# The attention scores' second pass on half the array's rows, both components at once, with the order of four engines written out

## The chip, the cores and the metric

The kernel runs on one core of one Trainium2 chip. The metric is the time of one execution in microseconds on the device; the median of the runs counts. TensorE (PE) multiplies matrices into PSUM, VectorE (DVE) and ScalarE (ACT) read PSUM, GpSimd (POOL) works on SBUF alone, and SyncE (SP) issues most transfers. Each engine has its own queue and takes its instructions in order; semaphores tie the queues together.

## What is computed

The reference is one encoder layer. The change touches its differential attention: four heads, each with two components c of 64 query and key features, 2048 tokens, values of 128 features.

```python
def block(args):
    q_blk, start = args
    ...
    bias = -slopes[:, None, None] * dist
    s = jnp.einsum('bhcqd,bhckd->bhcqk', q_blk, k).astype(jnp.float32) * scale
    p = jax.nn.softmax(s + bias[None, :, None], axis=-1)
    a = p[:, :, 0] - lam[None, :, None, None] * p[:, :, 1]
    return jnp.einsum('bhqk,bhkd->bhqd', a.astype(v.dtype), v)
```

Around it stand the input projection, a retention branch, the output projection with a residual and a two-layer MLP; none of these is edited.

## The kernel before, in words

Numbers are carried as a high and a low part, both of the type fp32r. A product of two such numbers is made of the high-high, high-low and low-high terms.

The attention stage handles 64 tiles i of 128 queries, 16 to a head; two tiles make a group g of 256 queries. Each tile goes through a pipeline of functions that is called slot by slot, four slots to a tile, in the loop at the end of `encoder`:

- `load_keys` (L971) brings a head's keys into `ka`, for each component the 64 rows of the high part in partitions 0 to 63 and those of the low part in 64 to 127. `load_group` (L993) brings the queries: `qa` holds the high part in both halves of the partitions, `qb` the low part in both halves.
- `scores` (L1023) makes, in each of a tile's four slots, the scores of one component c against 1024 keys: two matmuls on `qa` (L1042), which give high-high and high-low in one pass over 128 rows, and two on `qb` (L1043), low-high and low-low. DVE then adds the distance bias and takes the running minimum of a row (L1047; the queries are negated, so that the minimum belongs to the largest score), and after a component's second half ACT takes the exponential with its sum (L1059).
- `combine` (L1062) makes the ratio of the two sums times lambda on DVE (L1068 to L1070), and has POOL scale the second component (L1074) and add it to the first (L1075), 1024 keys at a time.
- `turn` (L1228) transposes the combined weights of tile i-2, a quarter per slot: four PE transposes into a PSUM tile `pa` (L1236), then `split_psum`: ACT writes the high part (L55), DVE the low part (L56).
- `weigh` (L1241) multiplies values and transposed weights for a group, two key tiles per slot, three matmuls each (L36 to L38 in `mm3`), into the PSUM tile `po`; after a group's eighth slot ACT copies `po` to `oT` (L1254).
- `turn_back` (L1257) transposes `oT` back into a `pa` buffer (called `pz`), scales it on ACT (L1265) and stores it.

In a slot the loop (L1272) calls `scores` for tile i, `turn` for tile i-2, `weigh` for the group of tiles i-4 and its neighbour, in even tiles' slot 1 `turn_back`, and in slot 3 `combine`. PE's order is the order of these calls (`manual_schedule` with PE alone); DVE, ACT and POOL are ordered by the planner. Of the eight PSUM banks the scores have two tiles of two banks, `po` two tiles and `pa` two.

The first two tiles (LEAD) are scored inside the retention stage before (`lead_scores`, L1080), on one-bank tiles between the retention's own matmuls: some of these use 64 rows of the array (`ret.scores`, L532, shown as 64*128), some 64 columns (`ret.within` L548, `ret.across` L560, shown as 128*64). There PE, DVE and ACT follow the order of the calls.

Of the kernel before, what the change touches and what calls it, by code (L numbers as in the profile page):

```python
# [8 lines left out]
F32 = mybir.dt.float32  # L9
# [8 lines left out]
P = 128  # L18
# [567 lines left out]
def encoder(ctx: ExitStack, tc: tile.TileContext, a: dict, out: bass.AP, dbg=None):  # L586
# [406 lines left out]
    def load_group(g):  # L993
        h, qs = g // (S // QG), g % (S // QG) * QG
        qa = kp_.tile([P, 2, QG], F32R, tag="qa", name="qa")
        qb = kp_.tile([P, 2, QG], F32R, tag="qb", name="qb")
        for t, s in ((qa, qh_d), (qb, ql_d)):
            for half in range(2):
                d = nc.sync.dma_start(
                    t[half * 64 : half * 64 + 64].bitcast(F32),  # L1000
                    s[h][:, qs : qs + QG].rearrange("(c d) q -> d c q", d=64).bitcast(F32),
                )
# [20 lines left out]
    def scores(i, slot, banks):  # L1023

        c, hf = divmod(slot, 2)
# [4 lines left out]
        if slot == 0:  # L1030
            tiles[i] = dict(p=[], l=[])
        if hf == 0:
            tiles[i]["p"].append(hp.next([P, S], F32, "p"))
            tiles[i]["nm"] = kp_.tile([P, 4], F32, tag="nm", name="nm", bufs=8)
        p, nm = tiles[i]["p"][c], tiles[i]["nm"]
        ql = slice(qi * P, qi * P + P)
        w = 1024 // len(banks)
        for b, sc in enumerate(banks):
            for o in range(0, w, 512):
                k0 = hf * 1024 + b * w + o  # L1040
                r = ka[:, c, k0 : k0 + 512]
                nc.tensor.matmul(sc[:, o : o + 512], qa[:, c, ql], r, start=True, stop=False)  # L1042
                nc.tensor.matmul(sc[:, o : o + 512], qb[:, c, ql], r, start=False, stop=True)  # L1043
            n = hf * len(banks) + b
            k0 = hf * 1024 + b * w
            b0 = k0 + S - P - qt * P
            nc.vector.tensor_tensor_reduce(  # L1047
                out=p[:, k0 : k0 + w],
                in0=sc[:],
                in1=bias[:, b0 : b0 + w],  # L1050
                scale=1.0,
                scalar=nm[:, n - 1 : n] if n else 3.0e38,
                op0=ALU.add,
                op1=ALU.min,
                accum_out=nm[:, n : n + 1],
            )
        if hf == 1:
            l = kp_.tile([P, 1], F32, tag="l", name="l", bufs=12)
            nc.scalar.activation(p[:], p[:], AF.Exp, bias=nm[:, n : n + 1], scale=-1.0, accum_out=l[:])  # L1059
            tiles[i]["l"].append(l)  # L1060

    def combine(i):  # L1062

        g, qi = divmod(i, 2)
        h = i // NT
        ps_, ls_ = tiles[i]["p"], tiles[i]["l"]
        ratio = kp_.tile([P, 1], F32, tag="ratio", name="ratio", bufs=6)
        nc.vector.reciprocal(ratio[:], ls_[1][:])  # L1068
        nc.vector.tensor_scalar(ratio[:], ratio[:], ls_[0][:], nlam[:, h : h + 1], op0=ALU.mult, op1=ALU.mult)  # L1069
        nc.vector.reciprocal(groups[g]["rl"][:, qi : qi + 1], ls_[0][:])  # L1070
        for k2 in range(2):
            p0, p1 = (t[:, k2 * 1024 : (k2 + 1) * 1024] for t in ps_)
            e = nc.vector if k2 == 0 and i == NI - 1 else nc.gpsimd
            e.tensor_scalar(p1, p1, ratio[:], 1.0, op0=ALU.mult, op1=ALU.mult)  # L1074
            e.tensor_tensor(out=p0, in0=p0, in1=p1, op=ALU.add)  # L1075
# [2 lines left out]
    LEAD = 2  # L1078

    def lead_scores(n):  # L1080
        i, slot = divmod(n, 4)
        scores(i, slot, [ret.bank([P, 512], "sc") for _ in range(2)])
        if slot == 3:
            combine(i)


# [134 lines left out]
    with ExitStack() as ph:  # L1221
        pools.append(ph.enter_context(pool(tc, "att_l", 2, side="right")))
        ap2 = ph.enter_context(pool(tc, "att_a", 2, side="right"))
        ps_s = ph.enter_context(pool(tc, "ps_as", 2, PSUM))
        ps_v = ph.enter_context(pool(tc, "ps_av", 2, PSUM))
        ps_t = ph.enter_context(pool(tc, "ps_at", 2, PSUM))

        def turn(i, k4):  # L1228
            g, qi = divmod(i, 2)
            p0 = tiles[i]["p"][0]  # L1230
            if qi == 0:
                groups[g]["a"][k4] = [ap2.tile([P, 4, QG], F32R, tag=n, name=n, bufs=7) for n in ("aTh", "aTl")]
            pa = ps_t.tile([P, 4, P], F32, tag="pa", name="pa")
            for j in range(4):
                kt = k4 * 4 + j
                nc.tensor.transpose(pa[:, j], p0[:, kt * P : (kt + 1) * P], ident[:])  # L1236
            qq = slice(qi * P, qi * P + P)
            th, tl = groups[g]["a"][k4]
            split_psum(nc, th[:, :, qq], tl[:, :, qq], pa[:])

        def weigh(g, slot):  # L1241

            h, qs = g // (S // QG), g % (S // QG) * QG
            vh, vl = heads[h]["v"]
            if slot == 0:
                groups[g]["po"] = ps_v.tile([P, QG], F32, tag="po", name="po")
# [5 lines left out]
            if slot == 7:  # L1252
                oT = ap2.tile([P, QG], F32, tag="oT", name="oT")
                nc.scalar.activation(oT[:], po[:], AF.Copy)  # L1254
                groups[g]["oT"] = oT

        def turn_back(g):  # L1257
            h, qs = g // (S // QG), g % (S // QG) * QG
# [8 lines left out]
            nc.scalar.dma_start(os.rearrange("(t p) d -> p t d", p=P), ot[:])  # L1267

        LT, LV = 2, 4
        ph.enter_context(tc.manual_schedule(engines={mybir.EngineType.PE}))  # L1270
        load_values(0)
        for i in range(LT, NI):  # L1272
            for slot in range(4):
                if slot == 0 and i % NT == 0 and i < NI - 4:
                    hh = (i + NT - 1) // NT
                    with tc.issue_after(groups[8 * hh - 4]["loaded"].ins):
                        load_keys(hh)
                        load_values(hh)
# [6 lines left out]
                j = i - LV  # L1285
                if 0 <= j:
# [23 lines left out]
        def ws(*slots):  # L1310
            for slot in slots:
                weigh(g - 1 + slot // 8, slot % 8)

        places = (hp.next([P, 2, DM], F32R, "wo") for _ in range(6))
        parts = [norms(tt, eg[:, 2], eg[:, 2]) for tt in (0, 4)]
        turn(NI - 2, 0)
        turn(NI - 2, 1)
        ws(0, 1)
        turn_back(g - 2)
        combine(NI - 1)  # L1320
        ws(2, 3)
        ph.enter_context(tc.manual_schedule(engines=ENGINES))
        turn(NI - 2, 2)
        next(parts[0])
        ws(4)
# [336 lines left out]
```

## Time and profile before

| | |
|---|---|
| median of 3 runs | 2817.68 us |
| lowest and highest | 2817.52 and 2819.99 us |
| profiled execution, time | 2819.93 us |
| profiled execution, span of its instructions | 2818.2 us |
| mean granted TensorE clock | 0.982 |
| attention stage, first and last score matmul in it | about 799 to 1339 us after the start |

Times inside the profile count from its first instruction. In its rows stand the engine, the line of the kernel, what is written from what, the shape (rows*columns of the array, then the moving operand) and, in groups, the busy time, the mean duration of one in ns, and the idle time before them with what ended it. Matmul durations overlap: what one costs is the distance between starts.

### The profile page before, as it was taken

To read this page: it belongs to the slowest core of one execution; us is meant where nothing else is said; L and a number is where in the kernel's file an instruction comes from. 1 tells how busy PE (TensorE), PEld (TensorE's weight loads), DVE (VectorE), ACT (ScalarE), POOL (GpSimd) and SP (SyncE) were. 2 spreads that over 40 slices of the span, in tenths; PEclk is the share of its full clock that TensorE was granted. 3 is DMA by queue.
4 is the path that set the end of the run, shared out by engine and by line. 5 is a ranking of instruction groups with operands and counts; after the bars stand their busy time and mean duration, and the time that the engine had idled before them with its cause. 6 is when DMAs were issued, how large, how long until landed. Compare 5 with 4: busy or idle time off the path is not lost.

```text
span 2818.2 us, 41052 instructions
## 1 busy us (share of the span) xinstructions
PE 2716.7 (96%) x15488; PEld 2332.3 (83%) x15488; DVE 1906.4 (68%) x2883; ACT 1298.4 (46%) x1844; POOL 1329.9 (47%) x768
## 2 busy tenths in 40 slices
PE   6998999998889999999899999999999999999999
PEld 4898989997778888888777788888888888888887
DVE  7888864787779999999888466665556435435542
ACT  5344422343467777777533245544445332222221
POOL 4235232513357777888454366765565104323320
PEclk8999999999899999999999999999999999999999
DMA  3665673259433222221378768776445848755471
GB/s 127 186 202 159 233 283 113 90 190 261 120 89 79 63 73 67 69 98 53 133 226 274 272 219 256 243 262 243 157 149 181 288 170 302 274 190 178 158 246 45
DMA packets 361030, 494.51 MB, mean 175 GB/s; under 512 B 23168, under 2 KB 257152, under 8 KB 352640
## 3 DMA queue, kind: packets, MB, share of 16 engines
q1 hardware_dynamic: 338608, 466.71, 50.5%
q10 hardware_dynamic: 21648, 20.98, 2.2%
q0 software_dynamic: 576, 4.19, 0.4%
q8 instruction: 122, 2.00, 0.3%
q14 instruction: 76, 0.62, 0.1%
HBM read 315.64 MB, written 176.16 MB: 175 GB/s over the span
## 4 chain that ended last, share of the span: by engine, by line
PE 79%; DVE 7%; DMA 2%; issue 1%; ACT 1%; POOL 1%; SPq 0%; ACTq 0%; DVEq 0%; POOLq 0%
PE ps L38 11%; PE ps L36 11%; PE ps L37 11%; PE p L38 7%; PE p L36 7%; PE p L37 7%; PE pa L1236 4%; PE sc L1042 4%; PE sc L1043 4%; PE po L36 2%; PE po L38 2%; PE po L37 2%; DVE kvs L511 1%; PE mm L38 1%; PE mm L37 1%
## 5 line engine op out<-in xcount | busy, mean ns | idle before, releaser
L37 PE MATMUL p<-wl,ah 128*128 128x512 f32 x896 | 348.5, 389 | 0.0
L36 PE MATMUL p<-wh,ah 128*128 128x512 f32 x896 | 348.4, 389 | 0.0
L293 POOL TENSOR_TENSOR s<-raw 128x1024 f32<-128x1024 f32 x58 | 147.2, 2539 | 372.1 <-DMA raw<-in_w_in 102.8
L334 DVE TENSOR_TENSOR c<-ps,c 128x512 f32<-128x512 f32 x360 | 238.4, 684 | 116.1 <-PE ps L38 112.5
L50 DVE TENSOR_TENSOR wl<-s,wh 128x1024 fp32r<-128x1024 f32 x120 | 194.8, 1625 | 172.9 <-ACT wh L44 172.8
L1075 POOL TENSOR_TENSOR p<-p 128x1024 f32<-128x1024 f32 x127 | 303.5, 2415 | 0.1
L44 ACT ACTIVATE ah<-ra 128x1024 fp32r<-128x1024 f32 x112 | 112.6, 1052 | 412.7 <-PE p L37 410.8
L1059 ACT ACTIVATE p<-p,nm 128x2048 f32<-128x2048 f32 x128 | 256.9, 2007 | 36.8 <-DVE nm L1047 35.7
L50 DVE TENSOR_TENSOR ah<-ra,ah 128x1024 fp32r<-128x1024 f32 x76 | 103.4, 1396 | 218.8 <-ACT ah L44 218.8
L1485 POOL TENSOR_TENSOR c<-c 128x512 f32<-128x512 f32 x128 | 196.5, 1560 | 111.3 <-ACT c L1488 109.5
L38 PE MATMUL p<-wh,ah 128*128 128x512 f32 x608 | 236.5, 389 | 0.0
L1546 POOL TENSOR_TENSOR t<-br 128x1024 f32<-128x1024 f32 x32 | 77.3, 2417 | 335.9 <-DMA br<-in_w_mlp 172.2
L44 ACT ACTIVATE wh<-s 128x1024 fp32r<-128x1024 f32 x120 | 126.6, 1057 | 208.3 <-PE ps L37 107.5
L1042 PE MATMUL sc<-ka,qa 128*128 128x512 f32 x512 | 207.5, 405 | 3.2 <-ACT yt L575 2.7
L1074 POOL TENSOR_SCALAR p<-p,ratio 128x1024 f32<-128x1024 f32 x127 | 141.9, 1130 | 143.3 <-DVE ratio L1069 110.5
L1043 PE MATMUL sc<-ka,qb 128*128 128x512 f32 x512 | 203.0, 397 | 0.0
L37 PEld LDWEIGHTS p<-wl,ah 128*128 128x128 f32 x896 | 168.2, 188 | 35.0
L36 PEld LDWEIGHTS p<-wh,ah 128*128 128x128 f32 x896 | 168.2, 188 | 34.9
L55 ACT ACTIVATE aTh<-pa 128x512 fp32r<-128x512 f32 x256 | 151.0, 591 | 81.8 <-PE pa L1236 80.6
L1047 DVE CUSTOM_DVE_ANT_0 p<-sc,bias,nm 128x1024 f32<-128x1024 f32 (+1 forms) x136 | 167.7, 1233 | 22.6 <-PE sc L1043 21.0
L1236 PEld LDWEIGHTS pa<-ident,p 128*128 128x128 f32 x1024 | 120.3, 141 | 64.6 <-issue 30.2
L56 DVE TENSOR_TENSOR aTl<-pa,aTh 128x512 fp32r<-128x512 f32 x256 | 170.3, 686 | 3.8 <-DMA vh<-vhd 3.0
(376 smaller groups left out, 8131.2 us busy)
## 6 DMA issues: line engine op xcount, KB each, us to landing
br<-in_w_mlp SPq DMA_DIRECT2D x88, 512.0 KB, 5.5
raw<-in_w_mlp SPq DMA_DIRECT2D x32, 1024.0 KB, 5.9
raw<-in_w_in SPq DMA_DIRECT2D x28, 1024.0 KB, 5.9
xt<-in_x SPq DMA_DIRECT2D x20, 512.0 KB, 5.8
q<-rqd SPq DMA_DIRECT2D x16, 512.0 KB, 10.1
qa<-qhd SPq DMA_DIRECT2D x64, 128.0 KB, 3.0
qb<-qld SPq DMA_DIRECT2D x64, 128.0 KB, 3.0
ua11d<-c SPq DMA_DIRECT2D x32, 256.0 KB, 3.5
```

Of the source, the lines that this page charges most:

```text
L36: nc.tensor.matmul(out, ah, bh, start=first, stop=False)
L37: nc.tensor.matmul(out, ah, bl, start=False, stop=False)
L38: nc.tensor.matmul(out, al, bh, start=False, stop=last)
L44: nc.scalar.activation(hi, src, AF.Copy)
L50: e.tensor_tensor(out=lo, in0=src, in1=hi.bitcast(F32), op=ALU.subtract)
L334: nc.vector.tensor_tensor(out=o[:], in0=x0[:], in1=x1[:], op=op)
L1042: nc.tensor.matmul(sc[:, o : o + 512], qa[:, c, ql], r, start=True, stop=False)
L1043: nc.tensor.matmul(sc[:, o : o + 512], qb[:, c, ql], r, start=False, stop=True)
L1059: nc.scalar.activation(p[:], p[:], AF.Exp, bias=nm[:, n : n + 1], scale=-1.0, accum_out=l[:])
L1075: e.tensor_tensor(out=p0, in0=p0, in1=p1, op=ALU.add)
L1236: nc.tensor.transpose(pa[:, j], p0[:, kt * P : (kt + 1) * P], ident[:])
L1485: nc.gpsimd.tensor_tensor(out=u[n][:], in0=u[x0][:], in1=u[x1][:], op=op)
```

## The change

- Keys: for component 1 the halves are exchanged, so that its high part lies in partitions 64 to 127 (and the low part in 0 to 63). Component 0 stays.
- Queries: `qb` now holds the low part once, component 0 in partitions 0 to 63 and component 1 in 64 to 127, loaded by one transfer.
- `scores` handles both components of 1024 keys at once, in slots 0 and 2 only. The first pass is as before, over 128 rows. The second pass uses 64 rows of `qb` and of `ka`, component 0 the lower and component 1 the upper ones, alternating; it makes low-high alone, and the low-low term is gone.
- The exponentials are a function of their own (`exps`): component 1 in slot 3, component 0 in slot 1 of the next tile, followed there by `combine`. The reciprocal for the ratio (`inverse`) comes in slot 0 of the next tile, the ratio's multiplication moves from DVE to POOL, and the reciprocal `rl` moves into `turn`.
- `turn` is one slot later; in slots 0 and 2 the low part on DVE is called only after the scores.
- PSUM: `pa` has three buffers; the two `po` are the halves of one tile `pos` in one bank. The copy to `oT` is a function `away`, called at the end of an odd tile's slot 3, behind that tile's `exps(i, 1)`.
- DVE, ACT and POOL also follow the order of the calls through the whole stage.

```diff
         for c in range(2):
-            rs = slice(c * 64, c * 64 + 64)
-            d = nc.sync.dma_start(ka[0:64, c].bitcast(F32), kh_d[h][rs, :].bitcast(F32))
-            nc.sync.dma_start(ka[64:128, c].bitcast(F32), kl_d[h][rs, :].bitcast(F32))
+            rs, os = slice(c * 64, c * 64 + 64), slice(64 - c * 64, 128 - c * 64)
+            nc.sync.dma_start(ka[rs, c].bitcast(F32), kh_d[h][rs, :].bitcast(F32))
+            nc.sync.dma_start(ka[os, c].bitcast(F32), kl_d[h][rs, :].bitcast(F32))
...
+        for c, sc in enumerate(banks):
             for o in range(0, w, 512):
-                k0 = hf * 1024 + b * w + o
-                r = ka[:, c, k0 : k0 + 512]
-                nc.tensor.matmul(sc[:, o : o + 512], qa[:, c, ql], r, start=True, stop=False)
-                nc.tensor.matmul(sc[:, o : o + 512], qb[:, c, ql], r, start=False, stop=True)
+                nc.tensor.matmul(sc[:, o : o + 512], qa[:, c, ql], ka[:, c, k0 + o : k0 + o + 512], start=True, stop=False)
+        for o in range(0, w, 512):
+            for c, sc in enumerate(banks):
+                rs = slice(c * 64, c * 64 + 64)
+                nc.tensor.matmul(sc[:, o : o + 512], qb[rs, 0, ql], ka[rs, c, k0 + o : k0 + o + 512], start=False, stop=True)
...
-        nc.vector.tensor_scalar(ratio[:], ratio[:], ls_[0][:], nlam[:, h : h + 1], op0=ALU.mult, op1=ALU.mult)
-        nc.vector.reciprocal(groups[g]["rl"][:, qi : qi + 1], ls_[0][:])
+        ratio = tiles[i]["r"]
+        nc.gpsimd.tensor_scalar(ratio[:], ratio[:], ls_[0][:], nlam[:, h : h + 1], op0=ALU.mult, op1=ALU.mult)
...
-        ps_v = ph.enter_context(pool(tc, "ps_av", 2, PSUM))
-        ps_t = ph.enter_context(pool(tc, "ps_at", 2, PSUM))
+        ps_v = ph.enter_context(pool(tc, "ps_av", 1, PSUM))
+        pos = ps_v.tile([P, 2, QG], F32, tag="po", name="po")
+        ps_t = ph.enter_context(pool(tc, "ps_at", 3, PSUM))
...
-        ph.enter_context(tc.manual_schedule(engines={mybir.EngineType.PE}))
+        ph.enter_context(tc.manual_schedule(engines=ENGINES | {mybir.EngineType.Pool}))
...
-                if i >= LEAD:
-                    scores(i, slot, [ps_s.tile([P, 1024], F32, tag="sc", name="sc")])
-                if 0 <= i - LT:
-                    turn(i - LT, slot)
+                low, (t, k4) = [], divmod(4 * (i - LT) + slot - 1, 4)
+                if t >= 0:
+                    turn(t, k4, low)
                 j = i - LV
+                if 0 < j and j % 2 == 0 and slot == 1:
+                    turn_back(j // 2 - 1)
+                if slot % 2 == 0:
+                    scores(i, slot // 2, [ps_s.tile([P, 1024], F32, tag="sc", name="sc") for _ in range(2)])
+                for f in low:
+                    f()
+                if slot == 0 and i > LEAD:
+                    inverse(i - 1)
                 if 0 <= j:
                     weigh(j // 2, j % 2 * 4 + slot)
-                if 0 < j and j % 2 == 0 and slot == 1:
-                    turn_back(j // 2 - 1)
-                if slot == 3 and LEAD <= i < NI - 1:
-                    combine(i)
+                if slot == 1 and i > LEAD:
+                    exps(i - 1, 0)
+                    combine(i - 1)
+                if slot == 3:
+                    exps(i, 1)
+                if 0 <= j and j % 2 and slot == 3:
+                    away(j // 2)
```

The lead-in calls the same `scores` on one-bank tiles, four parts to a tile, and both exponentials, `inverse` and `combine` after the fourth. Behind the loop the last tile's `exps`, its `inverse` and the last quarter of tile NI-3 are called ahead of what stood there.

More of the change, by code (lines that the diff above doesn't have):

```diff
@@ L996, in load_group @@
         qb = kp_.tile([P, 2, QG], F32R, tag="qb", name="qb")
[L997 to L1002, printed above, removed]
+        nc.sync.dma_start(qb[:, 0].bitcast(F32), ql_d[h][:, qs : qs + QG].bitcast(F32))
+        for half in range(2):
+            d = nc.sync.dma_start(
+                qa[half * 64 : half * 64 + 64].bitcast(F32),
+                qh_d[h][:, qs : qs + QG].rearrange("(c d) q -> d c q", d=64).bitcast(F32),
+            )
         groups[g] = dict(loaded=d, q=(qa, qb), a=[None] * 4, rl=kp_.tile([P, 2], F32, tag="rl", name="rl", bufs=6), po=None)
@@ L1021, in first_bias, with scores @@
         nc.vector.tensor_scalar(o, o, SLOPES[0], None, op0=ALU.mult)
-    def scores(i, slot, banks):
-        c, hf = divmod(slot, 2)
+    def scores(i, n, banks):
         g, qi = divmod(i, 2)
@@ L1029, in scores @@
         qa, qb = groups[g]["q"]
[L1030 to L1035, printed above, removed]
+        if n == 0:
+            tiles[i] = dict(
+                p=[hp.next([P, S], F32, "p") for _ in range(2)], l={},
+                nm=[kp_.tile([P, 4], F32, tag="nm", name="nm", bufs=8) for _ in range(2)],
+            )
         ql = slice(qi * P, qi * P + P)
-        w = 1024 // len(banks)
-        for b, sc in enumerate(banks):
+        w = banks[0].shape[1]
+        k0 = n * w
+        for c, sc in enumerate(banks):
             for o in range(0, w, 512):
-                k0 = hf * 1024 + b * w + o
-                r = ka[:, c, k0 : k0 + 512]
[L1042 to L1046, printed above, removed]
+                nc.tensor.matmul(sc[:, o : o + 512], qa[:, c, ql], ka[:, c, k0 + o : k0 + o + 512], start=True, stop=False)
[3 more added lines that the diff above has]
+                nc.tensor.matmul(sc[:, o : o + 512], qb[rs, 0, ql], ka[rs, c, k0 + o : k0 + o + 512], start=False, stop=True)
+        b0 = k0 + S - P - qt * P
+        for c, sc in enumerate(banks):
+            p, nm = tiles[i]["p"][c], tiles[i]["nm"][c]
             nc.vector.tensor_tensor_reduce(
@@ L1056, in scores, with exps, inverse @@
             )
[L1057 to L1060, printed above, removed]
+        tiles[i]["n"] = n
+    def exps(i, c):
+        l = kp_.tile([P, 1], F32, tag="l", name="l", bufs=12)
+        p, n = tiles[i]["p"][c], tiles[i]["n"]
+        nc.scalar.activation(p[:], p[:], AF.Exp, bias=tiles[i]["nm"][c][:, n : n + 1], scale=-1.0, accum_out=l[:])
+        tiles[i]["l"][c] = l
+    def inverse(i):
+        tiles[i]["r"] = kp_.tile([P, 1], F32, tag="ratio", name="ratio", bufs=6)
+        nc.vector.reciprocal(tiles[i]["r"][:], tiles[i]["l"][1][:])
     def combine(i):
@@ L1080, in lead_scores @@
     def lead_scores(n):
-        i, slot = divmod(n, 4)
-        scores(i, slot, [ret.bank([P, 512], "sc") for _ in range(2)])
-        if slot == 3:
+        i, part = divmod(n, 4)
+        scores(i, part, [ret.bank([P, 512], "sc") for _ in range(2)])
+        if part == 3:
+            exps(i, 1)
+            inverse(i)
+            exps(i, 0)
             combine(i)
@@ L1224, in encoder, with turn @@
         ps_s = ph.enter_context(pool(tc, "ps_as", 2, PSUM))
-        ps_v = ph.enter_context(pool(tc, "ps_av", 2, PSUM))
-        ps_t = ph.enter_context(pool(tc, "ps_at", 2, PSUM))
-        def turn(i, k4):
+        ps_v = ph.enter_context(pool(tc, "ps_av", 1, PSUM))
+        pos = ps_v.tile([P, 2, QG], F32, tag="po", name="po")
+        ps_t = ph.enter_context(pool(tc, "ps_at", 3, PSUM))
+        def turn(i, k4, low=None):
             g, qi = divmod(i, 2)
             p0 = tiles[i]["p"][0]
+            if k4 == 0:
+                nc.vector.reciprocal(groups[g]["rl"][:, qi : qi + 1], tiles[i]["l"][0][:])
             if qi == 0:
@@ L1237, in turn @@
             qq = slice(qi * P, qi * P + P)
-            th, tl = groups[g]["a"][k4]
-            split_psum(nc, th[:, :, qq], tl[:, :, qq], pa[:])
+            th, tl = (t[:, :, qq] for t in groups[g]["a"][k4])
+            nc.scalar.activation(th, pa[:], AF.Copy)
+            f = lambda: nc.vector.tensor_tensor(out=tl, in0=pa[:], in1=th.bitcast(F32), op=ALU.subtract)
+            if low is None:
+                f()
+            else:
+                low.append(f)
         def weigh(g, slot):
@@ L1245, in weigh @@
             if slot == 0:
-                groups[g]["po"] = ps_v.tile([P, QG], F32, tag="po", name="po")
+                groups[g]["po"] = pos[:, g % 2]
             po = groups[g]["po"]
@@ L1251, in weigh, with away @@
                 mm3(nc, po[:], vh[:, kt], vl[:, kt], th[:, j], tl[:, j], kt == 0, kt == NT - 1)
[L1252 to L1255, printed above, removed]
+        def away(g):
+            oT = ap2.tile([P, QG], F32, tag="oT", name="oT")
+            nc.scalar.activation(oT[:], groups[g]["po"][:], AF.Copy)
+            groups[g]["oT"] = oT
         def turn_back(g):
@@ L1312, in ws @@
                 weigh(g - 1 + slot // 8, slot % 8)
+                if slot % 8 == 7:
+                    away(g - 1 + slot // 8)
         places = (hp.next([P, 2, DM], F32R, "wo") for _ in range(6))
         parts = [norms(tt, eg[:, 2], eg[:, 2]) for tt in (0, 4)]
+        exps(NI - 1, 0)
+        inverse(NI - 1)
+        turn(NI - 3, 3)
         turn(NI - 2, 0)
@@ L1321, in encoder @@
         ws(2, 3)
-        ph.enter_context(tc.manual_schedule(engines=ENGINES))
         turn(NI - 2, 2)
```

4 lines of the change are left out of this document (2 added, 2 removed).

## Prediction

> **What bounds the kernel now.** I read the page first (span, busy shares, chain), then the windows through the attention stage, the timeline of TensorE inside one slot, the groups of that stage by shape, and the waits.
>
> ```profile
> span 2818.2 us, 41052 instructions
> PE 79%; DVE 7%; DMA 2%; issue 1%; ACT 1%; POOL 1%; SPq 0%; ACTq 0%; DVEq 0%; POOLq 0%
> ```
>
> ```profile
> core 0: us, PE busy (x) PEld busy (x) DVE busy (x) ACT busy (x) POOL busy (x), PEclk, DMA share, GB/s
> 900.00:1000.00 100.00, 99.29 (x655) 85.07 (x654) 90.39 (x172) 77.34 (x110) 80.43 (x47) 1.00 0.31 82
> 1000.00:1100.00 100.00, 99.31 (x654) 84.86 (x653) 90.60 (x172) 77.32 (x110) 79.39 (x46) 1.00 0.12 38
> ```
>
> The chain that ended last is four fifths TensorE. In the attention stage PE is busy 99.3 us of 100 at the full granted clock, and VectorE is close behind with 90.4. So a shorter PE sequence is worth something only while nothing else becomes late, and VectorE has a tenth to give, no more.
>
> The read-out of the weighted values (oT) runs once per pair of query tiles, which gives the period:
>
> ```profile
> L1254 ACT ACTIVATE oT<-po x30: 383/384/388, 836.0 to 1340.6; 128x256 f32<-128x256 f32 x30
> ```
>
> 29 periods in 504.6 us are 17.40 us for two tiles, eight slots. One slot on PE, the head of the next one as its last row:
>
> ```profile
> 1003.74 0.40 PE L1042 MATMUL sc<-ka,qa 128*128 128x512 f32 x1
> 1003.97 0.40 PE L1043 MATMUL sc<-ka,qb 128*128 128x512 f32 x1
> 1004.21 0.39 PE L1042 MATMUL sc<-ka,qa 128*128 128x512 f32 x1
> 1004.44 0.40 PE L1043 MATMUL sc<-ka,qb 128*128 128x512 f32 x1
> 1004.67 0.60 PE L1236 MATMUL pa<-ident,p 128*128 128x128 f32 x4
> 1005.02 0.36 PE L36 MATMUL po<-aTh,vh 128*128 128x256 f32 x1
> ...
> 1005.82 0.39 PE L1042 MATMUL sc<-ka,qa 128*128 128x512 f32 x1
> ```
>
> The starts tell the price, not the durations, which overlap: a score matmul of 512 columns takes 0.233 us (four from 1003.74 to 1004.67), the four transposes 0.43 (to 1005.02 and the 0.08 by which that first record is longer than its 0.28 brothers), the six value matmuls 0.72, a slot 2.08. Eight slots are 16.64 us, the two transposes of the turned-back output about 0.22 more; the remaining 0.54 us of the 17.40 are waits and the changes of head.
>
> **Removed.** Per two slots (half a tile) the second pass has four full matmuls; afterwards four half-row ones in two pairs. If a pair costs one step, 2 x 0.233 = 0.465 us go per half, 1.86 per pair of tiles, 31 x 1.86 = 57.7 us in all. That half-row matmuls do run together is in this trace, in retention:
>
> ```profile
> 700.06 0.66 PE L470 MATMUL rt<-ident,kT 128*128 128x128 f32 x4
> 700.65 1.16 PE L532 MATMUL rS<-q,kT 64*128 64x128 f32 x16
> ```
>
> Four full-height ones need 0.66 us; a record lasts 0.27, so their step is about 0.11 to 0.13. Sixteen of half height, alternating between the two row halves and two PSUM banks just as the change does it, need 1.16: less than 0.06 each once the 0.27 of the last and the late start of the first (below) are taken off. Two run for the price of one. These are plain fp32; fp32r pairs are not in the trace, and that is rival 2.
>
> **Added: two changes of array shape per half.** Each slot's PE work is now all 128*128. In the lead-in the same fp32r score matmuls stand beside matmuls of another shape:
>
> ```profile
> 783.99 0.39 PE L1043 MATMUL sc<-ka,qb 128*128 128x512 f32 x1
> 784.31 1.09 PE L548 MATMUL ry<-sd,v 128*64 128x128 f32 x16
> 785.34 0.50 PE L1042 MATMUL sc<-ka,qa 128*128 128x512 f32 x1
> ```
>
> Into the other shape: 0.32 us from start to start instead of 0.233, 0.09 lost. Out of it: the last of the sixteen starts at about 784.31 + 1.09 - 0.27 = 785.13, the next at 785.34, 0.21 where a pair's step is 0.11, 0.10 lost; and that matmul's record is 0.50 instead of 0.40, because its weights were not loaded ahead, 0.10 more. I charge the same 0.10 to the way in, as its weights have 128 columns too. Sum: 0.19 in, 0.20 out, 0.39 per half. The retention rows agree: 700.06 + 0.66 - 0.27 = 700.45 to 700.65 is 0.20, 0.09 over the step. What is left is 0.465 - 0.39 = 0.075 per half, 0.30 per pair of tiles, 31 x 0.30 = 9.3 us. The bounds are 0 (free change, 57.7 us gained) and 0.5; the rows lie at 0.39 and I take that.
>
> The page "TensorE: Matmul & The Clock Gate" of the Trainium skill (Part 3, Measured speedup vs the span model) gives a pack of tiles the time of one matmul and about 4 ns for each further tile, with no term for entering or leaving the shape; by it the 57.7 us would all come (rival 3). The rows above show the missing term.
>
> **Added: waits.** Durations of the other engines in this stage:
>
> ```profile
> L1075 POOL TENSOR_TENSOR p<-p 128x1024 f32<-128x1024 f32 x42 | 100.2, 2409 | 0.0
> L1059 ACT ACTIVATE p<-p,nm 128x2048 f32<-128x2048 f32 x42 | 84.3, 2007 | 9.3 <-DVE nm L1047 8.8 <-DVE ratio L1069 0.5
> L56 DVE TENSOR_TENSOR aTl<-pa,aTh 128x512 fp32r<-128x512 f32 x84 | 55.8, 686 | 0.1
> L1047 DVE CUSTOM_DVE_ANT_0 p<-sc,bias,nm 128x1024 f32<-128x1024 f32 x41 | 52.5, 1280 | 6.4 <-PE sc L1043 6.4
> L1047 DVE CUSTOM_DVE_ANT_0 p<-sc,bias 128x1024 f32<-128x1024 f32 x42 | 51.2, 1219 | 1.4 <-PE sc L1043 0.2
> L55 ACT ACTIVATE aTh<-pa 128x512 fp32r<-128x512 f32 x82 | 48.4, 591 | 26.7 <-PE pa L1236 26.7
> L1074 POOL TENSOR_SCALAR p<-p,ratio 128x1024 f32<-128x1024 f32 x42 | 46.8, 1126 | 36.9 <-DVE ratio L1069 36.9
> L1265 ACT ACTIVATE ot<-pz,rl 128x128 f32<-128x128 f32 x20 | 6.3, 365 | 3.6 <-PE pz L1262 3.6
> L1069 DVE TENSOR_SCALAR ratio<-ratio,l,nlam 128x1 f32<-128x1 f32 x21 | 5.7, 273 | 0.7
> L1254 ACT ACTIVATE oT<-po 128x256 f32<-128x256 f32 x10 | 3.9, 386 | 1.1
> ```
>
> Call T the moment at which the scores of a half land. PE reaches the next T after two slots less the removed plus the changes: 4.16 - 0.465 + 0.39 = 4.08 us. Both components' scores now land together, so DVE does its two reductions one after the other, then ACT its exponential.
>
> First wait, the output accumulator. Both groups' po are now halves of one tile in one bank. In the second half of an odd tile ACT's fixed order is exps(i,1), then away(g). After T: 2 x 1.28 (reductions), 2.01 (exponential), 0.39 (oT) is 4.96, with hand-offs 5.0 us. PE issues weigh(g+1, slot 0) right behind the next scores, at T + 4.08. If it may not write the bank while ACT reads it, it stands still for 0.9 us, and the transposes and scores behind it in its queue stand too; DVE and ACT wait for those.
>
> Second wait, pa. Three buffers instead of two, but the low part of slot 0's transpose is now queued on DVE behind both reductions: it is done 2 x 1.22 + 0.69 = 3.1 us after T (0.1 to 0.2 sooner where instructions overlap). In an even tile slot 0, slot 1 and the turned-back output hold all three, so slot 2's transposes must wait. PE gets there at T + 0.72 + 0.43 + 0.22 + 0.72 = 2.1: a wait of 0.8 to 1.0 us. The other way to a free buffer leads through ACT, where the turned-back output is read behind the late exponential and oT (0.9 after T), two copies of 0.591 and its own two of 0.365: 2.8 us, no earlier. In the odd tile the buffer asked for has long been free.
>
> Both waits fall into the same even tile, and the first covers the second (PE comes 0.9 later, at 3.0). So one wait of about 0.9 us per pair stands whether or not the first exists: 30 x 0.9 = 27 us. Of the old 0.54 some 0.15 lies in the same place and is absorbed, 30 x 0.15 = 4.5 us back.
>
> The page "PSUM — Partial Sum Buffer" of the Trainium skill (PSUM bank collisions raise a hardware error) asks for a semaphore per bank and quadrant, not per address; by that rule the first wait exists. No run so far has two engines on halves of one bank; the sum holds without it.
>
> **Moved or free.** The ratio's multiplication goes from DVE (0.273) to POOL, 0.1 to 0.3 us there by my estimate from that row and 64 times; POOL is 80% busy and has 3.5 us (1126 + 2409 ns) to the first half of a combined tile, which lands about 1 us before slot 1's transposes ask for it a tile later, so I cost it at nothing; without that cover it would be up to 64 x 0.3 = 19 us. The reductions, splits and reciprocals on DVE make 7.8 - 0.27 = 7.5 us per tile (0.904 of 8.7), under the new 8.9, and no bound. load_group issues three DMAs on SP's queue instead of four, of the same bytes or fewer, a pair ahead: nothing. The lead-in has eight parts that lose one step and gain two changes, 8 x 0.16 = 1.3 us at most, in a stretch where PE has idle time. At the end both exponentials of the last tile follow its last scores, but PE has over 10 us of transposes and value matmuls queued before it needs them.
>
> **Sum.** -9.3 + 27 - 4.5 + 1 = +14 us against the profiled execution, whose span is 2818.2 and whose own time is 2819.9 us; the median of the three runs is 2817.7, so the forecast is 2817.7 + 14 = 2832 us, 0.5% slower. Its own range: with a wait of 0.65 the sum is about +6 (2824), with 1.4 (ACT's path frees the buffer, later) about +30 (2848).
>
> **Rivals.**
> 1. No new wait, faster. If oT is read within 4.1 us of T and the low part within 2.1 (DVE or ACT starting earlier than I place them), PE's sequence alone decides: -9.3 us, and up to -26 if the old 0.54 us per pair goes as well (31 x 0.54 = 17). For it: PE at 99.3% and all others under 91%. Against it: the two sums above, 5.0 against 4.08 and 3.1 against 2.1. Value 2806, range 2791 to 2810.
> 2. fp32r pairs do not run together, so the change doesn't do what it says: 57.7 us come back; PE then reaches its next T at 4.55 and the wait shrinks to 0.45. -9.3 + 57.7 + 30 x 0.45 - 4.5 = +57, 2875. Against it: the fp32 pairs.
> 3. The change of shape is free for row halves, as the page on the clock gate has it: PE needs 1.86 less per pair, but T to T is then 3.69 and the wait 1.3; -57.7 + 39 - 4.5 = -23, 2795. Against it: three rows with 0.09 to 0.21.
>
> **How the numbers follow.** Forecast 0.60; rival 1 0.27; rival 2 0.05; rival 3 0.08. What a measurement of this kernel can tell from no change is about 0.2%, 5.6 us. Of the forecast 0.05 lies within that and 0.55 above it, of rival 1 0.04 lies within. Faster 0.23 + 0.08 = 0.31, same 0.05 + 0.04 = 0.09, slower 0.55 + 0.05 = 0.60. Both signs hold much, so the range reaches from 2795 (rival 3, and most of rival 1) to 2850 (the forecast's own end); left out are rival 2 and the tails, under 0.2.
>
> **What would show it.** Starts of the two members of a pair under 0.02 us apart and a step of about 0.23 between pairs (rival 2: 0.23 inside the pair). First pair 0.32 or more after the last full score matmul, and the value matmul after the last pair about 0.4 after it. A gap of about 0.9 us on PE once per two tiles, in even tiles, ended by ACT oT or, at slot 2's transposes, by DVE aTl. A period of about 17.9 us between oT read-outs; 17.1 or less makes the forecast wrong. DVE should fall a little below 90%, PE to about 94%. If PE is still 99% busy and the period shorter, the waits were the failed step; if the period is longer and PE full, the pairs were.

## The result, and the profile after

The changed kernel takes 2833.8 us (median of four runs, 2830.6 to 2834.8), the kernel before 2817.6 in the runs beside it: the ratio is 1.0055, with a 95% interval of 1.0043 to 1.0068. It is 16 us slower where 14 were forecast. The profiled execution is the fastest of the four (span 2828.8), that of before was the slowest of its own, so the two traces differ by 10.6 us only.

The page of the changed kernel, and the same two windows of the attention stage:

```profile
span 2828.8 us, 41062 instructions
...
PE 44%; DVE 3%; DMA 1%; POOL 1%; issue 1%; ACT 0%; SPq 0%; DVEq 0%; POOLq 0%; ACTq 0%
```

```profile
900.00:1000.00 100.00, 94.06 (x636) 74.04 (x634) 83.86 (x157) 75.25 (x107) 82.42 (x56) 1.00 0.28 71
1000.00:1100.00 100.00, 94.06 (x641) 74.68 (x639) 85.10 (x158) 74.84 (x108) 85.00 (x58) 1.00 0.11 31
```

PE is busy 94.1 us of 100 instead of 99.3, at the same full clock. No other engine is over 85.1, so nothing else has become the bound; something makes PE wait. (The chain back from the end now breaks off elsewhere and shows less of the span; it is not used here.)

Whom PE waits for, between 860 and 1300 us (in total, times, longest), in the changed kernel; PEld is PE's loading of weights, PE its matmuls:

```profile
PEld sc L1045 <- issue: 35.1, 96, 0.4
PEld po L36 <- ACT oT L1275: 34.5, 25, 1.4
...
PEld po L36 <- issue: 27.0, 74, 0.4
PE po L36 <- ACT oT L1275: 23.6, 25, 1.0
```

Two things are new. Ahead of every half-row pass (L1045) and of the value matmuls behind it (L36) the weight loads stand still for some 0.37 us: the change of shape. And once per pair of tiles the first value matmul waits 0.94 us for ACT's read-out oT. One such place on the timeline, from the rows of PE, DVE and ACT:

```profile
1004.35 1.28 DVE L1049 CUSTOM_DVE_ANT_0 p<-sc,bias,nm 128x1024 f32<-128x1024 f32 x1 [0.28 <-PE sc L1045]
...
1005.56 1.28 DVE L1049 CUSTOM_DVE_ANT_0 p<-sc,bias,nm 128x1024 f32<-128x1024 f32 x1
...
1006.59 1.17 PE L1040 MATMUL sc<-ka,qa 128*128 128x512 f32 x4
...
1006.95 2.01 ACT L1064 ACTIVATE p<-p,nm 128x2048 f32<-128x2048 f32 x1 [0.64 <-DVE nm L1049]
1007.69 0.73 PE L1045 MATMUL sc<-ka,qb 64*128 64x512 f32 x4
...
1008.95 0.36 ACT L1275 ACTIVATE oT<-po 128x256 f32<-128x256 f32 x1
...
1009.37 0.38 PE L36 MATMUL po<-aTh,vh 128*128 128x256 f32 x1 [0.94 <-ACT oT L1275]
```

Read it as the chain of the forecast: the scores land at 1004.35, two reductions, the exponential and oT follow in a row until 1009.31, 4.96 us later; PE has been ready since 1009.37 - 0.94 = 1008.43, 4.08 us after the landing. The four half-row matmuls (second last PE row) start within 0.73 - 0.39 = 0.34 us of each other. That is one step of 0.233 between two pairs and the 0.10 that the way into the shape costs; one after the other they would need three steps.

The read-outs, whose distance is the period of two tiles, up to the 29th, before and after:

```profile
L1254 ACT ACTIVATE oT<-po x29: 383/385/388, 836.0 to 1323.0; 128x256 f32<-128x256 f32 x29
```

```profile
L1275 ACT ACTIVATE oT<-po x29: 359/362/368, 830.7 to 1329.6; 128x256 f32<-128x256 f32 x29
```

28 periods last 487.0 us before and 498.9 after, 17.39 and 17.82 us each. The account of the two traces: the first read-out comes 5.3 us earlier (836.0 to 830.7), the 28 periods add 11.9, and from the 29th read-out to the end it takes 2828.8 - 1329.6 = 1499.2 instead of 1495.2, 4.0 more. That makes the 10.6. Not all of the 5.3 belongs to the change. The first score matmul of the lead-in, before and after, stands at 778.4 and 775.6:

```profile
L1042 PE MATMUL sc<-ka,qa x512: 389/396/792, 778.4 to 1338.8; 128*128 128x512 f32 x171
```

```profile
L1040 PE MATMUL sc<-ka,qa x512: 387/397/504, 775.6 to 1341.7; 128*128 128x512 f32 x171
```

So 2.8 us are gone before the first edited matmul runs, in stages that are the same in both kernels; in the traces of the experiments this moment lies anywhere between 772.2 and 779.7. What the change can have saved there is 2.5.

### The profile page after: what moved, and what is told of

Its sections match the earlier page's. It is cut to its first block, busy times and chain, and to the rows that moved or that the text cites. A ratio compares the mean times of both kernels' runs of the same rounds, so it can differ in the third digit from the quotient of the medians.

```text
span 2828.8 us, 41062 instructions
## 1 busy us (share of the span) xinstructions
PE 2695.2 (95%) x15488; PEld 2276.2 (80%) x15488; DVE 1878.3 (66%) x2819; ACT 1294.9 (46%) x1844; POOL 1358.8 (48%) x832
## 4 chain that ended last, share of the span: by engine, by line
PE 44%; DVE 3%; DMA 1%; POOL 1%; issue 1%; ACT 0%; SPq 0%; DVEq 0%; POOLq 0%; ACTq 0%
PE p L37 7%; PE p L38 7%; PE p L36 7%; PE ps L38 7%; PE ps L36 7%; PE ps L37 7%; DMA mx<-mixd 1%; PE mm L38 1%; PE mm L36 1%; PE mm L37 1%; DVE hl L50 0%; POOL c L1521 0%; DVE quads L181 0%; PE htp L178 0%; DVE xt L1431 0%
## 5 line engine op out<-in xcount | busy, mean ns | idle before, releaser
L36 PE MATMUL p<-wh,ah 128*128 128x512 f32 x896 | 348.4, 389 | 0.0
L50 DVE TENSOR_TENSOR wl<-s,wh 128x1024 fp32r<-128x1024 f32 x120 | 186.6, 1556 | 172.0 <-ACT wh L44 172.0
L36 PE MATMUL po<-aTh,vh 128*128 128x256 f32 x512 | 168.0, 328 | 31.4 <-ACT oT L1275 31.4
L36 PEld LDWEIGHTS p<-wh,ah 128*128 128x128 f32 x896 | 168.2, 188 | 35.0
L1049 DVE CUSTOM_DVE_ANT_0 p<-sc,bias 128x1024 f32<-128x1024 f32 (+1 forms) x128 | 149.5, 1205 | 33.2 <-PE sc L1045 26.6
L36 PEld LDWEIGHTS po<-aTh,vh 128*128 128x128 f32 x512 | 97.1, 190 | 77.4 <-ACT oT L1275 44.2
L1251 PE MATMUL pa<-ident,p 128*128 128x128 f32 x1024 | 154.6, 274 | 3.7 <-POOL p L1083 1.6
```

What stands on the lines that cost most here:

```text
L36: nc.tensor.matmul(out, ah, bh, start=first, stop=False)
L50: e.tensor_tensor(out=lo, in0=src, in1=hi.bitcast(F32), op=ALU.subtract)
L1049: nc.vector.tensor_tensor_reduce(out=p[:, k0 : k0 + w], in0=sc[:], in1=bias[:, b0 : b0 + w], scale=1.0, scalar=nm[:, n - 1 : n] if n else ...
```

## The experiments

All ratios are to the kernel before, run beside each, with their 95% intervals. Theory A is that of the prediction: the change of shape eats most of what the pairs save, and waits decide the sign. The rivals differ by experiment. Where an expectation speaks of the first kernel it means the one with the first wait undone; its fourth kernel is the one with both waits undone, called "the version without the two waits" here.

**Undoing the first wait.** In an odd tile's last slot the read-out goes ahead of the exponential.

```diff
+                if 0 <= j and j % 2 and slot == 3:
+                    away(j // 2)
                 if slot == 3:
                     exps(i, 1)
-                if 0 <= j and j % 2 and slot == 3:
-                    away(j // 2)
```

> In an odd tile's last slot ACT reads the output accumulator ahead of the exponential instead of behind it; nothing else differs from the changed kernel. Theory A (PE's longer wait is for that read, a second one for the third transpose buffer stands right behind it): the gap of 0.94 us on PE at the first value matmul of an even tile is gone, and one of 0.6 to 0.9 us appears at slot 2's transposes of the same tile, ended by DVE's low part; the period of two tiles falls from 17.8 to about 17.6 us and the time by 3 to 10 us, to 2824 to 2831. Theory B (only the read-out is late): no new gap, the whole 0.94 us is won 30 times, 28 us: 2806.

Measured: 2811.9 us, 0.9986 (0.9977 to 0.9995): some 20 us less (22 by the medians, 19 by the two ratios) by moving one 0.38 us instruction, and just faster than before. The mechanism is A's, the size nearer B's:

```profile
PEld pa L1251 <- ACT ot L1286: 12.4, 26, 0.5
...
PE pa L1251 <- ACT ot L1286: 7.2, 26, 0.3
```

```profile
L1275 ACT ACTIVATE oT<-po x29: 384/384/387, 830.6 to 1309.6; 128x256 f32<-128x256 f32 x29
```

The second wait is there, 26 times, at the third transpose buffer, but it is ended by ACT's reading of the turned-back output and holds the transposes for 0.4 to 0.5 us (0.28 of it as idle time of PE) instead of 0.6 to 0.9. A period is 479.0 / 28 = 17.11. One such place, from the rows of DVE, ACT and PE:

```profile
986.79 1.23 DVE L1049 CUSTOM_DVE_ANT_0 p<-sc,bias 128x1024 f32<-128x1024 f32 x1 [0.51 <-PE sc L1045]
...
988.53 0.62 ACT L1286 ACTIVATE ot<-pz,rl 128x128 f32<-128x128 f32 x2
...
989.20 0.66 PE L1251 MATMUL pa<-ident,p 128*128 128x128 f32 x4 [0.28 <-ACT ot L1286]
```

The scores land at 986.79 and ACT's reading ends at 989.15, 2.4 us later. With the read-out early, ACT is early too, and its way to a free buffer is the shorter of the two.

**Undoing the second wait as well.** Beside the edit above, DVE makes the low part of an even tile's slot 0 between the two reductions.

```diff
             nc.vector.tensor_tensor_reduce(
...
             )
+            if c == 0:
+                for f in mid:
+                    f()
...
+                    mid = []
+                    if slot == 0 and i % 2 == 0 and j > 0:
+                        low, mid = [], low
```

> As the first kernel, and in even tiles' slot 0 DVE makes the low part between the two reductions instead of behind them. Theory A (the second wait is for this buffer): both gaps are gone; the second reduction ends 0.65 us later, which may hold the next scores for 0.2; the period falls to 16.7 to 17.0 us, 24 to 33 us less: 2801 to 2810, below the kernel before. Theory B (the period is set by what the other engines need, or by the second reduction's delay): no faster than the first kernel, 2824 or above.

Measured: 2808.9 us, 0.9974 (0.9964 to 0.9984): 23 to 25 us under the changed kernel and the fastest version so far. The period is 475.6 / 28 = 16.99 with the changes of head, and 16.87 for most pairs. Its waits and its window (columns as in the first windows):

```profile
PEld sc L1040 <- DVE nm L1049: 11.8, 26, 1.0
```

```profile
900.00:1300.00 400.00, 397.51 (x2682) 311.98 (x2684) 351.93 (x662) 317.80 (x448) 348.78 (x236) 1.00 0.24 67
```

PE is full again, 397.5 us of 400. The gain came out at the small end of A. The late second reduction does hold the next scores, as A had feared: 11.8 us over 26 times in weight loads that stand still.

**Undoing the half rows in the new order.** Keys and queries are laid out as before and the second pass takes 128 rows.

```diff
-                rs = slice(c * 64, c * 64 + 64)
-                nc.tensor.matmul(sc[:, o : o + 512], qb[rs, 0, ql], ka[rs, c, k0 + o : k0 + o + 512], start=False, stop=True)
+                nc.tensor.matmul(sc[:, o : o + 512], qb[:, c, ql], ka[:, c, k0 + o : k0 + o + 512], start=False, stop=True)
```

> The order of the changed kernel with the second pass on all 128 rows again (keys and queries laid out as before, the low-low term back). Theory A (two changes of the array's shape cost 0.39 us per half tile and the pairs save 0.465): PE's sequence grows by 0.075 us per half, 0.30 per pair of tiles, of which the wait hides 0.08: 0.22 x 30 = 7 us, 2841. Theory B (the change of shape is free, the lost time is all waits): 0.465 per half, 1.86 per pair, of which one wait hides up to 0.465: 1.4 x 30 = 42 us, 2876.

Measured: 2850.2 us, 1.0122 (1.0106 to 1.0137). Within the stage A is right:

```profile
L1274 ACT ACTIVATE oT<-po x29: 361/363/367, 831.7 to 1337.0; 128x256 f32<-128x256 f32 x29
```

505.3 / 28 = 18.05 us, 0.23 over the changed kernel's 17.82, where A had 0.22 and B 1.4. The time grew by 16 and not by 7 because the rest behind the stage was about 9 us longer in this run (2845.2 - 1337.0 = 1508.2 instead of 1499.2). The trace has the 9 us in one place. This is the third hundred of microseconds behind the 29th read-out, in this run and then in the changed kernel:

```profile
1537.00:1637.00 100.00, 92.90 (x393) 74.13 (x392) 54.02 (x116) 29.89 (x53) 35.91 (x24) 0.91 0.72 259
```

```profile
1529.60:1629.60 100.00, 96.04 (x430) 77.16 (x429) 56.47 (x116) 29.95 (x54) 33.60 (x22) 1.00 0.75 272
```

PE gets through 37 matmuls fewer, which at 0.233 us each is 8.6 us (an estimate), and the granted clock is 0.91 instead of 1.00. What lowered it stays open; it is not a cost of the full rows inside the stage.

The same edit on the version without the two waits:

> The fourth kernel (both waits taken away, TensorE full, 2809 us) with the second pass on all 128 rows again. Theory A (a way in and out costs 0.39 us per half, the pairs save 0.465): the period grows from 16.87 by up to 0.30 us to 17.1 to 17.2, 7 to 9 us in the attention stage, 2816 to 2818; what lies behind the stage may shift by some us more, as it did in the other full-row run. Theory B (the change of shape is free): up to 1.86 us per pair, less what waits hide, 40 us or more: 2849 and above. In either case the difference is what half rows are worth once nothing else waits.

Measured: 2813.6 us, 0.9990 (0.9981 to 0.9998), 4.6 us over the half-row version. Its read-outs run

```profile
L1277 ACT ACTIVATE oT<-po x29: 384/385/387, 831.2 to 1312.8; 128x256 f32<-128x256 f32 x29
```

that is 17.20 us against 16.99: half rows are worth 0.21 us per pair of tiles, 6 us of the stage, where 57.7 would be had without the change of shape. The prediction had 0.30; part of it may be hidden by the wait that is left. And 17.20 is itself 0.19 under the 17.39 of the kernel before: that part of the gain comes from the rest of the change (order, calls and buffers), without any half rows.

**Doubling the change of shape.** Per half, both components' first 512 keys, their pair, the next 512, their pair.

```diff
-        for c, sc in enumerate(banks):
-            for o in range(0, w, 512):
+        for o in range(0, w, 512):
+            for c, sc in enumerate(banks):
...
-        for o in range(0, w, 512):
             for c, sc in enumerate(banks):
...
```

> The same matmuls as the changed kernel in another order: first pass of 512 keys for both components, their pair, then the next 512, so four changes of the array's shape per half tile instead of two. Theory A (0.39 us for a way in and out): each half grows by 0.39 us, a pair of tiles by 1.56, of which the wait hides 0.39: 1.17 x 30 = 35 us, 2869. Theory B (the change of shape is free): the same time as the changed kernel, 2834.

Measured: 2888.7 us, 1.0255 (1.0241 to 1.0269), 55 us more than the changed kernel. B falls.

```profile
L1273 ACT ACTIVATE oT<-po x29: 357/363/367, 833.2 to 1384.2; 128x256 f32<-128x256 f32 x29
```

A period is 551.0 / 28 = 19.68 us, 1.86 over the changed kernel's, where A had 1.17. Most of the rest is a wait at the transposes that the expectation left out:

```profile
PEld pa L1249 <- issue: 12.5, 19, 0.7
...
PE pa L1249 <- DVE rl L1243: 9.2, 19, 0.5
```

It is not a new one. It stands in an even tile's slot 2, where the prediction put its second wait:

```profile
1010.45 1.22 DVE L1047 CUSTOM_DVE_ANT_0 p<-sc,bias 128x1024 f32<-128x1024 f32 x1 [1.02 <-PE sc L1043]
...
1012.74 0.69 DVE L1253 TENSOR_TENSOR aTl<-pa,aTh 128x512 fp32r<-128x512 f32 x1
...
1013.57 0.63 PE L1249 MATMUL pa<-ident,p 128*128 128x128 f32 x4 [0.49 <-DVE rl L1243]
```

The scores land at 1010.45, DVE ends the low part at 1013.43, with the reciprocal `rl` right behind it, and the transposes start 3.1 us after the landing, which is the prediction's figure for DVE's way to a free buffer. Here the first wait is down to 9.7 us in 22 times, 0.44 each, so it no longer covers the second.

**Is a pair really one step?** First by order: lower rows twice, then upper rows twice.

```diff
-        for o in range(0, w, 512):
-            for c, sc in enumerate(banks):
+        for c, sc in enumerate(banks):
+            for o in range(0, w, 512):
                 rs = slice(c * 64, c * 64 + 64)
```

> The changed kernel with the four half-row matmuls ordered by component: lower rows twice, then upper rows twice, so that only the middle two can run together. Theory A (a pair runs in one step's time): three steps instead of two, 0.233 us more per half, 0.93 per pair of tiles, of which the wait for the read-out hides 0.23: 0.70 x 30 = 21 us, 2855. Theory B (the pairs only start together, and the end of a record is modelled, so they don't really overlap): the same time as the changed kernel, 2834.

Measured: 2834.9 us, 1.0063 (1.0050 to 1.0075), no change. This looks like B, but the trace shows the four matmuls still in two steps:

```profile
1006.28 0.74 PE L1045 MATMUL sc<-ka,qb 64*128 64x512 f32 x4
1006.95 0.39 PE L36 MATMUL po<-aTh,vh 128*128 128x256 f32 x1
```

So either the order of issue doesn't bind the two row halves, or half-row matmuls overlap whatever their rows. The next run tells: the version without the two waits, with both components' second pass on rows 0 to 63.

```diff
-                rs = slice(c * 64, c * 64 + 64)
-                nc.tensor.matmul(sc[:, o : o + 512], qb[rs, 0, ql], ka[rs, c, k0 + o : k0 + o + 512], start=False, stop=True)
+                nc.tensor.matmul(sc[:, o : o + 512], qb[0:64, c, ql], ka[0:64, c, k0 + o : k0 + o + 512], start=False, stop=True)
```

> The fourth kernel (no waits, 2809 us) with the second pass of both components on rows 0 to 63, so the same half-row matmuls and changes of shape but nothing that could run together; the low-low term is left out as in the changed kernel. Theory A (two row halves run at the same time): four steps of 0.233 us instead of two, 0.465 per half, 1.86 per pair of tiles, 30 to 31 times: 56 us, 2865. Theory B (half height alone makes a matmul cheaper, or their records overlap without gain): no difference, 2809. By the one-by-one run alone (order by component, no change) A and B can't be told apart, since TensorE may have taken the upper rows ahead of time.

Measured: 2857.4 us, 1.0143 (1.0126 to 1.0160), 48 us more than the version it is made from; the period is 18.53 instead of 16.99.

```profile
1003.83 1.19 PE L1044 MATMUL sc<-ka,qb 64*128 64x512 f32 x4
1004.95 0.38 PE L36 MATMUL po<-aTh,vh 128*128 128x256 f32 x1
```

Four matmuls on one row half need 1.19 us, on two halves 0.73: 0.46 saved, two steps of 0.23. The ends of these records are modelled, but the starts say the same: from the first half-row matmul to the value matmul it is 1004.95 - 1003.83 = 1.12 us here, 1006.95 - 1006.28 = 0.67 in the run before, and 0.67 in the version without the two waits (its rows stand further down). A holds. Of its 1.86 per pair of tiles 1.54 came, and some 0.3 was hidden, at least in part because the scores wait less for the late reduction (3.8 us in weight loads instead of 11.8).

**Filling the last wait.** In even tiles' slot 2 half of the value matmuls goes between the two components' first passes.

```diff
         for c, sc in enumerate(banks):
+            if c and ahead is not None:
+                ahead()
             for o in range(0, w, 512):
                 nc.tensor.matmul(sc[:, o : o + 512], qa[:, c, ql], ka[:, c, k0 + o : k0 + o + 512], start=True, stop=False)
...
-            for kt in (2 * slot, 2 * slot + 1):
+            for kt in (2 * slot, 2 * slot + 1) if part is None else (2 * slot + part,):
...
+                    if slot == 2 and i % 2 == 0 and j >= 0:
+                        halfway = lambda: weigh(j // 2, j % 2 * 4 + slot, 0)
...
-                    weigh(j // 2, j % 2 * 4 + slot)
+                    weigh(j // 2, j % 2 * 4 + slot, 1 if slot == 2 and i % 2 == 0 else None)
```

> The fourth kernel; in even tiles' slot 2 half of the value matmuls goes between the first passes of the two components, so that PE has work while the late second reduction still holds component 1's banks. Theory A (that wait, some 0.4 us per pair, is real loss): the period falls from 16.87 to 16.5 to 16.6, 8 to 11 us: 2798 to 2801. Theory B (another wait takes its place, as the next half is shorter by the same work): 2806 to 2810.

Measured: 2809.4 us, 0.9973 (0.9962 to 0.9984), no gain. The wait has moved and not gone:

```profile
PEld sc L1042 <- DVE nm L1051: 11.4, 28, 0.4
```

11.4 us in total as before it was 11.8; the next half is shorter by the work that was taken out of it. The last step, the next head's bias made earlier on DVE, in the last slot of a head's last tile (beside the edit above):

```diff
-            bias = pools[h % 2].tile([P, BW], F16, tag="bias", name="bias", bufs=1)
-            nc.vector.tensor_scalar(bias[:], heads[h - 1]["bias"][:], SLOPES[h] / SLOPES[h - 1], None, op0=ALU.mult)
-            heads[h]["bias"] = bias
+            heads[h]["bias"] = biases[h]
...
+                if slot == 3 and i % NT == NT - 1 and i < NI - 1:
+                    next_bias(i // NT + 1)
```

> The one before, and the next head's bias is made on DVE behind the reductions of the last tile of a head instead of ahead of those of the first. Theory A (the long pair at a change of head, 17.9 instead of 16.87, is this 1.3 us instruction in the way): three pairs lose about 1 us each, 3 us: 2795 to 2798. Theory B (it is the new head's keys or something else): no difference.

Measured: 2810.2 us, 0.9973 (0.9963 to 0.9983), no difference. But this doesn't speak against A, because on DVE the edit moved the instruction past nothing. The bias stands right ahead of the new head's first reduction in the version that it is made from and in this run alike:

```profile
918.21 1.46 DVE L990 TENSOR_SCALAR bias<-bias 128x3968 f16<-128x3968 f16 x1
919.84 1.23 DVE L1051 CUSTOM_DVE_ANT_0 p<-sc,bias 128x1024 f32<-128x1024 f32 x1 [0.17 <-DVE bias L990]
```

```profile
915.74 1.43 DVE L996 TENSOR_SCALAR bias<-bias 128x3968 f16<-128x3968 f16 x1
917.34 1.23 DVE L1056 CUSTOM_DVE_ANT_0 p<-sc,bias 128x1024 f32<-128x1024 f32 x1 [0.17 <-DVE bias L996]
```

In the first of the two, the low parts ahead of the bias start at 917.01 and the reduction 2.83 us later; where no head changes the same distance is 987.25 - 985.44 = 1.81. The reduction comes 1.02 us late, and the pair at this change of head takes 17.80 us instead of the 16.87 of the next (read-outs at 916.65, 934.45 and 951.32). So the traces point at the bias instruction; a run that takes it out of the reduction's way is missing.

**The fixed order alone.** The kernel before, with DVE, ACT and POOL also in the order of the calls and nothing moved.

```diff
-        ph.enter_context(tc.manual_schedule(engines={mybir.EngineType.PE}))
+        ph.enter_context(tc.manual_schedule(engines=ENGINES | {mybir.EngineType.Pool}))
```

> The kernel before with one part of the change alone: DVE, ACT and POOL also in the order of the calls, nothing moved. Theory A (the calls had to be moved because in this order ACT's exponential stands ahead of the transposes' high part and DVE's low part waits for it): in every second slot DVE stands from the landing of the scores for 1.28 + 2.01 + 0.59 + 0.69 = 4.6 us, with the other slot about 6.6 us per half tile instead of 4.33, 9 us per pair, 30 x 9 = 270 us: about 3000 to 3100. Theory B (the planner's order is near the order of the calls): within 10 us of the kernel before.

Measured: 3157.9 us, 1.1208 (1.1189 to 1.1227). The wait that A named is the third of these, 2.4 us in the mean; the first two are what ACT and POOL then wait for:

```profile
ACT p L1059 <- DVE nm L1047: 197.7, 56, 4.8
POOL p L1074 <- DVE rl L1070: 192.0, 27, 8.9
DVE aTl L56 <- ACT aTh L55: 157.7, 66, 3.0
```

The size was under-estimated by about 60 us or more. One thing that A left out is the clock. A window of this run, in the columns used above:

```profile
1000.00:1100.00 100.00, 75.30 (x391) 62.45 (x392) 53.35 (x104) 46.25 (x67) 47.62 (x27) 0.82 0.25 64
```

PE is busy three quarters of the time, and its granted clock is 0.82 here, and between 0.82 and 0.91 in each 100 or 150 us from 900 to 1650 us, where the kernel before has 1.00 in its own stage. How much of the 60 us is the clock's is not told apart. The fixed order alone is thus a loss; the splitting of the calls (the exponentials, the late low parts) is what makes it bearable, and the version with full rows and both waits undone even gains the 0.19 us per pair above.

## Why the prediction was right, point by point

- **Two half-row matmuls for one step**: right. Four take 0.73 us on two row halves and 1.19 on one.
- **0.39 us for a way into the shape and out of it**: right. In the version without the two waits the last half-row matmul starts at 985.31 + 0.73 - 0.39 = 985.65 and the value matmul at 985.98, 0.33 instead of 0.233, with a record of 0.39 instead of 0.28. The way in is the same: 985.31 - 984.98 = 0.33, and 0.34 instead of 0.233 from the first pair to the second. Sum 0.40.

```profile
984.98 0.40 PE L1040 MATMUL sc<-ka,qa 128*128 128x512 f32 x1
985.31 0.73 PE L1045 MATMUL sc<-ka,qb 64*128 64x512 f32 x4
985.98 0.39 PE L36 MATMUL po<-aTh,vh 128*128 128x256 f32 x1
```

- **The first wait, 0.9 us from 5.0 against 4.08**: 0.94, from 4.96 against 4.08, with its cause shown by moving the read-out. The page "PSUM — Partial Sum Buffer" of the Trainium skill (PSUM bank collisions raise a hardware error) asks for a semaphore per bank and quadrant; the trace agrees as far as the program waits, 0.94 us, although PE and ACT use different halves of the bank. Whether the program's wait goes by the bank or by the one tile `pos`, and what would happen without it, no run here shows.
- **The second wait, covered by the first**: right; PE's weight loads have a gap of 0.16 us at slot 2's transposes beside the 0.94. DVE's way to a free buffer took the 3.1 us of the prediction in the run with four changes. But with the read-out moved, the wait was 0.4 to 0.5 instead of 0.8 to 1.0, since the buffer came free through ACT after 2.4 us. So "one wait of about 0.9 us per pair stands whether or not the first exists" did not hold there: the loss was half as large and the sum negative. For the case that the sentence had in mind, the read-out left in its place and no guard on the bank, there is no run; ACT would be at most 0.38 us later than in that run, so the wait would be between 0.4 and 0.8 us (an estimate). The forecast rests on the first wait, which does exist.
- **Sum per pair**: -0.30 + 0.90 - 0.15 = 0.45 forecast, 17.82 - 17.39 = 0.43 measured. By the periods of the runs its terms are -0.21 for the half rows (17.20 to 16.99), +0.83 for the two waits (16.99 to 17.82) and -0.19 for the rest of the change (17.39 to 17.20), so each was mis-sized by 0.04 to 0.09, and that the sum is off by only 0.02 is partly luck.
- **The ends of the stage**: both wrong, and that they nearly cancel is luck. I gave the lead-in at most +1.3; from its first score matmul to the first read-out it is 2.5 us shorter, and another 2.8 of the 5.3 had come in stages that the change doesn't touch. In the trace of before, from 798 to 822 us, DVE's low part stands 3.0 us behind the loading of the values and PE's transposes wait up to 3.3 for it; the changed kernel's trace has neither. Which part of the change removed it wasn't tried.

```profile
PE pa L1236 <- DVE aTl L56: 4.3, 2, 3.3
...
DVE aTl L56 <- DMA vh<-vhd: 3.0, 1, 3.0
```

And I gave the end nothing, with 10 us of PE work as cover; there the same shared bank stops PE once for 4.0 us, as the last group may not begin before the read-out of the one before it, which now stands late in ACT's fixed order:

```profile
PE po L36 <- ACT oT L1275: 4.0, 1, 4.0
```

The same 4.0 us still stand in the traces with the first wait and with both waits undone, whose edits are in the loop ahead of it; no run takes them away.

- **The ratio on POOL**: 0.335 us each, a little over the estimate; PE's list of waits between 860 and 1300 us has no POOL in it (DVE's has: 5.1 us, 10 times).
- **Rivals**: 2 fell with the one-side run, 3 with the four changes. Rival 3 took a model that has no term for the change of shape to say that the change is free; the run with four changes shows the term. Rival 1's value, 2806, is near what the kernel gives (2809) once both waits are taken out, so its condition was what failed. That the values agree doesn't show its price of 0.30 per pair: 0.21 comes from the half rows and 0.19 from the rest of the change.

## What to carry to other kernels

Price a packed matmul together with the way into its array shape and back: here 0.39 us per visit against 0.233 per saved step, so short visits of two saved steps leave almost nothing. When two buffers are put into one PSUM bank to free another, look at who reads the first half and what stands ahead of that read in its queue; here one copy behind an exponential cost some 20 us, and moving it turned a loss of 0.55% into a gain of 0.1%, of 0.26% with the next wait cut too. When a wait is removed, ask at once what is late next, and by which of its ways a buffer comes free first. And see in the trace that an edit moved what it was meant to move, before its time is taken as an answer.

## What the runs showed of the hardware that was not expected

The order of issue does not bind matmuls on different row halves. Issued as lower, lower, upper, upper, the four ran in 0.74 us, in pairs, like the alternating order (0.73), while four on the same half needed 1.19. The page "TensorE: Matmul & The Clock Gate" of the Trainium skill (Part 3, The mechanism) has matmuls start and end strictly in program order; the time measured here speaks against that for row halves, and the measurement decides. Which record belongs to which matmul the trace does not say, so the order inside the four is inferred from the times; and that they were issued in the order of the calls is taken from the kernel's `manual_schedule`, as no view shows the order of issue itself.
